# Small tiles for the scaled pairs, low parts by negated copies and accumulating loads, and folds of one block per step, in a decoder layer

## The chip, the cores and the metric

One core of one Trainium2 chip runs the whole layer in one launch. The metric is device time in microseconds (us). The kernel before has a median of 760.0 us over 3 runs (757.77 to 762.58).

## The reference

A decoder layer over 512 rows of 1024 columns, in fp32: an adaLN-modulated input, two causal attention branches (forgetting attention and stick-breaking attention), their gated merge and output projection, a norm, then a gated MLP (2816 wide) with a causal convolution of width 3, and a second norm. The change touches the part behind the first norm:

```python
u2 = x * (1.0 + sc2) + sh2
h = _causal_depthwise_conv(u2 @ w_up, conv_w, conv_b)
h_gate, h_val = jnp.split(h, 2, axis=-1)
ffn_out = (jax.nn.silu(h_gate) * h_val) @ w_down
x = _layer_norm(DEEPNORM_ALPHA * x + (1.0 + gt2) * ffn_out, ln2_g, ln2_b)
```

## The kernel before

**Split matmuls.** Each fp32 product is made of three matmuls on rounded parts: high by high, high by low, low by high. A weight tile arrives as fp32 (`raw`); ACT copies it rounded (the high part: `wh`, `wdh`), and DVE subtracts that from the original (the low part: `wl`, `wdl`, at L91).

**Items and the ring.** All weights of the layer's second half stand in one list of items (`add_item`), each with a source, a function that prepares it and its columns. `weights(i, ahead)` (L145 on) issues loads from SP in the list's order into a ring of 5 tiles `raw` (items of 512 columns, `rl`, go to a ring of 4 of their own in a late pool) and prepares `ahead` items beyond the one asked for. SP's order is the order of the code; the order of the other engines is made by a scheduler at build time. Each engine works through its own order strictly.

**Up projection.** A loop over 44 tiles n (L1097 on): 24 matmuls of 512 columns into one PSUM bank, which ACT (L1122) and DVE (L1123, L1124) evacuate together with the convolution. Six of the eight banks hold early products of the down projection, so two are left for this loop.

**Down projection.** It is a product of 2 x 2 blocks with seven multiplications (Strassen-like, in the Winograd form), over 11 pairs of 256 hidden channels. The rows of `wdp` hold the blocks of each pair as b11, b12, b22, b21 (512 columns each). Sums of weight blocks are formed by accumulating loads on POOL's queue (L160) and by `pair_proc`, and stored to DRAM as `t13`. B22 times the gate, the *scaled pairs*, is stored to DRAM as `wgt`: pairs 2 to 10 in `pair_proc` by an ACT DMA (L952), pairs 0 and 1 by two items of their own, listed at n = 17 and 21, that load 512 columns into a tile of the ring, multiply in place (L960, DVE) and store on POOL's queue (L961).

**The final stage** has four phases, each for both row blocks i = 0, 1 of the quadrant at hand: Z and then V (bank pairs `Z`, `W1`) over the two halves of `t13`; X over B21, whose six items are numbered 0 to 5 here (two pairs each, the last one pair); W over `wgt`: two streamed items for pairs 0 to 2, and eight *late items* (`rl`) for pairs 3 to 10, used by 24 matmuls of 512 columns for row block 2 and 48 of 256 columns for row block 3. Between them DVE *folds* the phases' banks into the residual `r` (tiles `xn`), times the gate halves `g0`, `g1`: `gated` (L1153 to L1155), called from `z_mark`, `v_mark`, `x_mark` and `w_mark` after each item. `first_rows` makes the second norm of row blocks 0 and 1 and stores them on POOL's queue (L1172); `tail` does so for blocks 2 and 3 at the end, with SP's stores.

Of the kernel before, what the change touches and what calls it, by code (L numbers as in the profile page):

```python
# [16 lines left out]
P = 128  # L17
# [6 lines left out]
FP = FT // 2  # L24
# [13 lines left out]
AHEAD = 2  # L38
NSPLIT = 3
LATE = 8  # L40
EARLY = 2
GS = 9
SS = 10
# [7 lines left out]
def layer_kernel(ctx: ExitStack, tc: tile.TileContext, out, xT, x, cT, crow, wa0, wa1, bcol, bgt, w1, wct, wv, bf,  # L51
# [18 lines left out]
    def nm(s):  # L70
        cnt[0] += 1
        return f"{s}_{cnt[0]}"
# [56 lines left out]
    def z(dt, s, shape=(P, 512)):  # L129
        return zp.tile(list(shape), dt, name=nm(s), tag="z", bufs=NZ)  # L130
# [8 lines left out]
    state = {"load": 0, "proc": 0}  # L139
    items, depth = [], [LOADS - 1]  # L140
    def add_item(src, proc, cols=1024):
        items.append([src, proc, cols, None, None])
        return len(items) - 1

    def weights(i, ahead=AHEAD):  # L145
        while state["load"] < min(len(items), i + depth[0]):
            it = items[state["load"]]
            if it[2] == 512:
                it[3] = state["late"].tile([P, 512], F32, name=nm("rl"), tag="rl", bufs=4)
            else:  # L150
                it[3] = stg.tile([P, 1024], F32, name=nm("raw"), tag="raw", bufs=LOADS)
            c = 0
            for src in it[0] if isinstance(it[0], list) else [it[0]]:
                w = src.shape[-1]
                d = nc.sync.dma_start(it[3][:, c : c + w], src)
# [210 lines left out]
    gated = []  # L366
# [202 lines left out]
    gt = [None, None]  # L569
# [81 lines left out]
    def split_cols(cols):  # L651
        def f(r):
            return split_proc(r, cols)
        return f
# [148 lines left out]
    last = hd[heads[1]]['last']  # L803
    for n, (b, h) in enumerate(heads):
        f1, f2, f3 = FILL[n // 8]
        if n + 2 < 16:
# [5 lines left out]
            last = hd[heads[n + 1]].get("last")  # L812
# [117 lines left out]
    def raw_proc(r):  # L930
        return r

    def halves_proc(r):
# [23 lines left out]

    def scale_proc(p):
        def f(r):
            V.tensor_tensor(r[:, 0:512], r[:, 0:512], gt[1][:, 512:1024], ALU.mult)  # L960
            G.dma_start(wgt[p], r[:, 0:512])  # L961
        return f

    wui, pi, wai = [], [], {}
# [22 lines left out]
    def add_late():  # L987
        if len(cli) < LATE:
            cli.append(add_item(wgt[FP - LATE + len(cli)], halves_proc, 512))

    def add_two(n, src, p, end):
        ws = [src(q) for q in range(p, min(p + 2, end))]
        n.append(add_item(ws, split_cols(512 * len(ws))))

    for p in range(0, FP - 1, 2):
        add_two(zi, lambda q: t13[q][:, 512:1024], p, FP - 1)
        if p == 0:
            add_pair_items(FP - 1)
            add_pair_sums(FP - 1)
    for p in range(0, FP - 1, 2):  # L1000
        add_two(vi, lambda q: t13[q][:, 0:512], p, FP - 1)
        if p > 2:
            add_late()
    for p in range(0, FP, 2):
        add_two(xi, lambda q: wdp[q][:, 1536:2048], p, FP)
        if p < 10:
            add_late()
# [27 lines left out]
    hs, ops, s4s = [], [], []  # L1035
# [61 lines left out]
    for n in range(2 * FT):  # L1097
        if n < NSPLIT:
            h, l = items[wui[n]][4]
# [41 lines left out]
    fin = ctx.enter_context(tc.tile_pool(name="fin", bufs=1, reuse_waits="tile"))  # L1141

    def fine(s):
        return fin.tile([P, 512], F32, name=nm(s), tag="fz", bufs=10)

    state["late"] = fin
    r = x1
    g0, g1 = gt[1][:, 0:512], gt[1][:, 512:1024]

    def half(w, e):  # L1150
        return [t[:, e * 512 : (e + 1) * 512] for t in w]

    def gated(i, e, t, src, op=ALU.add):  # L1153
        V.tensor_tensor(t, src, (g0, g1)[e], ALU.mult)
        V.tensor_tensor(r[i][e], r[i][e], t, op)  # L1155


    def stat_tile():
        return cons.tile([P, 3, 6], F32, name=nm("st"), tag="st3", bufs=2)
# [11 lines left out]
            V.scalar_tensor_tensor(v, v, rs, lnr[1][:, c], ALU.mult, ALU.add)  # L1171
            eng.dma_start(out[tb, c], v)  # L1172

    p1, u2, q1, u3, c22 = [[fine(n) for _ in range(2)] for n in ("p1", "u2", "q1", "u3", "c22")]

    def phase(ps, idx, end, take, mark, last=None):
        for n, k in enumerate(idx):
            w = weights(k)
            for a, p in enumerate(range(2 * n, min(end, 2 * n + 2))):
                t = take(p)  # L1180
                for i in range(2):
                    product(ps[i], t[:, top[i]], t[:, bot[i]], *half(w, a), p == 0, p == FP - 1)
            mark(n)
        if end < FP:
            t = take(end)
            for i in range(2):
                product(ps[i], t[:, top[i]], t[:, bot[i]], *[v[last] for v in state["t13"]], False, True)
            mark(len(idx))

    def g_part(c):  # L1190
        def f(p):
            t = ops[p][2][c]
            ops[p][2][c] = None
            return t
        return f

    def z_mark(n):
# [12 lines left out]
        if n < 5:  # L1210
            for p in range(max(GS, 2 * n + 2), min(FP, 2 * n + 4)):
                ready(p)

    def v_mark(n):
        for p in range(max(SS, 2 * n), min(FP, 2 * n + 2)):
            ops[p][3] = halves(ops[p][3])
        if n == 0:
            for i in range(2):
                V.tensor_tensor(q1[i], q1[i], Z[i], ALU.add)
                V.tensor_tensor(u3[i], u2[i], Z[i], ALU.add)  # L1220
        if n in (1, 2):
            gated(n - 1, 0, q1[n - 1], q1[n - 1])

    def first_rows(i):
        st = stat_tile()
# [16 lines left out]

    lnr = lnr2
    Z = [bank() for _ in range(2)]
    phase(Z, zi, FP - 1, g_part(0), z_mark, 1)
    W1 = [bank() for _ in range(2)]
    phase(W1, vi, FP - 1, g_part(1), v_mark, 0)
    X = [bank() for _ in range(2)]
    phase(X, xi, FP, lambda p: ops[p][1], x_mark)
# [101 lines left out]
```

## Time and profile before

| | |
|---|---|
| median of 3 runs | 760.0 us (757.77 to 762.58) |
| profiled execution | 760.22 us, its span 758.4 us, granted TensorE clock 0.996 |
| PE (matmuls) | 736.6 us busy, 97% of the span, 3478 matmuls |
| DVE | 608.5 us, 80% |
| ACT | 384.8 us, 51% |
| POOL | 108.5 us, 14% |
| DMA of the hardware queue for loads and stores | 37602 packets, 112.09 MB |
| DMA of POOL's queue | 2576 packets, 7.41 MB |

The span is what the profiler saw of the execution; 1.8 us lie around it. Rows of the profile name engine, line, operation and tiles as output<-inputs; a time in brackets at a row's end is the engine's idle time before it and what ended it. Rows of the waits give the waiting engine and line, what it waited for, us in total, the number of times, and the longest. Rows of stretches give, after the stretch, its length, the busy us of PE, its weight loads, DVE, ACT and POOL, then PE's granted clock, the share of time that DMA engines were busy, and GB/s.

### The profile page before, as it was taken

Reading aid. Unit: us, or ns where it says so; the run is one execution under the profiler, and the core shown is the slowest. Engines: PE = TensorE matmul, PEld = TensorE weight load, DVE = VectorE, ACT = ScalarE, POOL = GpSimd, SP = SyncE. Lnnn points to the kernel's source line nnn. Section 1 sums busy time; section 2 is a strip of 40 time slices with the busy share of each in tenths; the row PEclk is TensorE's granted clock in tenths of the full one; section 3 lists DMA queues with packets and bytes.
Section 4 is the critical chain, followed back from the end, with each engine's and each line's share of the span. In section 5 each row is a group of like instructions: output and inputs, shape, how many; then the busy total and the mean of one; then the engine's idle time right before and its main releaser. Section 6 shows DMA issues by size and latency. Waiting matters only on the chain.

```text
span 758.4 us, 9876 instructions
## 1 busy us (share of the span) xinstructions
PE 736.6 (97%) x3478; PEld 607.2 (80%) x3478; DVE 608.5 (80%) x1017; ACT 384.8 (51%) x678; POOL 108.5 (14%) x138
## 2 busy tenths in 40 slices
PE   8999999999999999999999999999899999999993
PEld 4878888878888888788889888877688888887883
DVE  6869799887888895864687889876886687669997
ACT  4566566685866654432055563443454355446530
POOL 1026223452010011462000000000000000000010
PEclk9999999999999999999999999999999999999998
DMA  9943446313432232542074777667774674567711
GB/s 323 406 174 116 162 168 219 114 58 119 161 112 82 86 128 78 183 144 83 1 250 111 259 227 233 198 193 208 246 234 159 193 223 144 167 189 249 225 68 56
DMA packets 43252, 128.01 MB, mean 169 GB/s; under 512 B 5665, under 2 KB 6177, under 8 KB 43202
## 3 DMA queue, kind: packets, MB, share of 16 engines
q1 hardware_dynamic: 37602, 112.09, 42.4%
q0 software_dynamic: 2576, 7.41, 5.0%
q10 hardware_dynamic: 3024, 7.88, 3.0%
q8 instruction: 27, 0.44, 0.2%
q14 instruction: 23, 0.19, 0.1%
HBM read 117.07 MB, written 10.22 MB: 168 GB/s over the span
## 4 chain that ended last, share of the span: by engine, by line
PE 66%; DVE 13%; DMA 12%; issue 6%; ACT 2%; SPq 0%; ACTq 0%; POOL 0%; DVEq 0%; POOLq 0%
PE ps L135 14%; PE ps L133 14%; PE ps L134 14%; PE ps L300 5%; DVE wl L91 3%; DMA raw<-in_wdp 3%; PE ps L551 2%; PE ps L533 2%; PE ps L892 2%; PE ps L891 2%; PE ps L893 2%; DMA raw<-in_wup 2%; DMA raw<-in_wa 1%; PE ps L1075 1%; PE ps L1076 1%
## 5 line engine op out<-in xcount | busy, mean ns | idle before, releaser
L91 DVE TENSOR_TENSOR wl<-raw,wh 128x1024 fp32r<-128x1024 f32 (+2 forms) x112 | 139.9, 1249 | 57.7 <-ACT wh L181 57.3
L181 ACT ACTIVATE wh<-raw 128x1024 fp32r<-128x1024 f32 (+1 forms) x103 | 108.4, 1053 | 138.0 <-PE ps L134 63.9
L133 PE MATMUL ps<-u2h,wh 128*128 128x512 f32 (+1 forms) x376 | 141.9, 377 | 2.6 <-DVE cv L1124 2.5
L135 PE MATMUL ps<-u2h,wl 128*128 128x512 f32 (+1 forms) x376 | 141.3, 376 | 0.0
L134 PE MATMUL ps<-u2l,wh 128*128 128x512 f32 (+1 forms) x376 | 141.2, 376 | 0.0
L133 PEld LDWEIGHTS ps<-u2h,wh 128*128 128x128 f32 x376 | 70.8, 188 | 17.5 <-issue 4.8
L135 PEld LDWEIGHTS ps<-u2h,wl 128*128 128x128 f32 x376 | 70.8, 188 | 12.9
L134 PEld LDWEIGHTS ps<-u2l,wh 128*128 128x128 f32 x376 | 70.8, 188 | 12.6
L133 PE MATMUL ps<-uh,wh 128*128 128x512 f32 x200 | 79.4, 397 | 0.0
L135 PE MATMUL ps<-uh,wl 128*128 128x512 f32 x200 | 78.3, 391 | 0.9 <-DVE wl L91 0.9
L134 PE MATMUL ps<-ul,wh 128*128 128x512 f32 x200 | 78.2, 391 | 0.0
L160 POOL DMA_DIRECT2D raw<-in_wdp x11 | 9.5, 865 | 271.8 <-DVE raw L946 96.1
L135 PEld LDWEIGHTS ps<-uh,wl 128*128 128x128 f32 x200 | 37.6, 188 | 9.5 <-DVE wl L91 1.4
L513 POOL TENSOR_TENSOR pt<-pt,om 128x127 f32<-128x127 f32 (+3 forms) x32 | 43.2, 1361 | 8.0 <-DVE om L512 8.0
L133 PEld LDWEIGHTS ps<-uh,wh 128*128 128x128 f32 x200 | 37.6, 188 | 7.3
L134 PEld LDWEIGHTS ps<-ul,wh 128*128 128x128 f32 x200 | 37.7, 188 | 7.2
L1122 ACT ACTIVATE cv<-ps,cw 128x512 f32<-128x512 f32 x44 | 33.5, 766 | 16.5 <-PE ps L135 10.4
L1123 DVE SCALAR_TENSOR_TENSOR cv<-ps,cw,cv 128x511 f32<-128x511 f32 x44 | 32.6, 744 | 5.4 <-ACT cv L1122 5.4
L1130 ACT ACTIVATE cv<-cv 128x512 f32<-128x512 f32 x22 | 13.9, 630 | 39.2 <-DVE cv L1124 39.2
L1124 DVE SCALAR_TENSOR_TENSOR cv<-ps,cw,cv 128x510 f32<-128x510 f32 x44 | 32.5, 742 | 0.2
L632 POOL TENSOR_TENSOR raw<-raw,gt 128x1024 f32<-128x1024 f32 x8 | 21.3, 2669 | 67.6 <-DMA raw<-in_wo 54.5
L512 DVE TENSOR_TENSOR_SCAN om<-om,dg 128x127 f32<-128x127 f32 (+3 forms) x32 | 29.6, 981 | 0.5 <-ACT om L507 0.4
(226 smaller groups left out, 1606.7 us busy)
## 6 DMA issues: line engine op xcount, KB each, us to landing
raw<-in_wup SPq DMA_DIRECT2D x44, 512.0 KB, 4.5
raw<-in_wa SPq DMA_DIRECT2D x32, 512.0 KB, 4.2
raw<-in_wct SPq DMA_DIRECT2D x25, 512.0 KB, 3.8
raw<-in_wdp SPq DMA_DIRECT2D x22, 512.0 KB, 5.5
wa<-in_wa SPq DMA_DIRECT2D x14, 512.0 KB, 7.9
raw<-in_wdp SPq DMA_DIRECT2D x24, 256.0 KB, 5.2
raw<-in_wdp POOLq DMA_DIRECT2D x11, 512.0 KB, 7.8
t<-raw ACTq DMA_DIRECT2D x10, 512.0 KB, 4.1
```

Of the source, the lines that this page charges most:

```text
L91: state["read"] = V.tensor_tensor(o, i, fl(hi), ALU.subtract)
L133: PE.matmul(ps, wh, ah, start=first, stop=False)
L134: PE.matmul(ps, wh, al, start=False, stop=False)
L135: return PE.matmul(ps, wl, ah, start=False, stop=last)
L181: state["hi"] = S.activation(h[:, 0:cols], r[:, 0:cols], AF.Copy)
L300: PE.matmul(grp[g], w, u, start=j == 0 and n == 0, stop=j == KT - 1 and n == (1 if g == 7 else 2))
L512: V.tensor_tensor_scan(d0, d0, dg[:, 513 - (e - s) : 512][:, ::-1], 0.0, ALU.mult, ALU.max)
L513: G.tensor_tensor(pt[b][:, s : e - 1], pt[b][:, s : e - 1], om[:, s + 1 : e], ALU.mult)
L632: G.tensor_tensor(r, r, gt[0], ALU.mult)
L1122: S.activation(t, ps, AF.Identity, bias=cw[:, n, 3:4], scale=cw[:, n, 2:3])
L1123: V.scalar_tensor_tensor(t[:, 1:], ps[:, 0:511], cw[:, n, 1:2], t[:, 1:], ALU.mult, ALU.add)
L1124: V.scalar_tensor_tensor(t[:, 2:], ps[:, 0:510], cw[:, n, 0:1], t[:, 2:], ALU.mult, ALU.add)
```

## The change

1. The two items of scaled pairs 0 and 1 are listed at n = 15 and 19, and load into tiles of 512 columns from the general pool (`z`), as all `rl` tiles now do. The late pool keeps 8 work tiles where it had 10.
2. For items 1, 3 and 5 of X and both streamed items of W, the low part is made in another way: ACT copies the rounded high part once more with the sign turned, and a DMA on POOL's queue loads the source again, adding to it. High and low parts get tiles of their own, `xh` and `xl`, two of each.
3. Folds go one block per step, each directly from its bank, and spread over more steps; they take 34 operations of 512 columns where there were 30.

The tuples SENT_V, SENT_W and HELD_Z are empty, and HELD_V and HELD_X place the late items where they were.

```diff
@@ weights
             if it[2] == 512:
-                it[3] = state["late"].tile([P, 512], F32, name=nm("rl"), tag="rl", bufs=4)
+                it[3] = z(F32, "rl")
@@ preparing an item
+    def sent_split(srcs):
+        def f(r):
+            cols = 512 * len(srcs)
+            h = state["fin"].tile([P, 1024], F32R, name=nm("xh"), tag="xh", bufs=2)
+            l = state["fin"].tile([P, 1024], F32R, name=nm("xl"), tag="xl", bufs=2)
+            hi_of(h[:, 0:cols], r[:, 0:cols])
+            S.activation(l[:, 0:cols], fl(h[:, 0:cols]), AF.Copy, scale=-1.0)
+            for a, src in enumerate(srcs):
+                G.dma_start(l[:, a * 512 : a * 512 + 512], src, accum_op=ALU.add)
+            return h, l
+        return f
...
     def scale_proc(p):
         def f(r):
-            V.tensor_tensor(r[:, 0:512], r[:, 0:512], gt[1][:, 512:1024], ALU.mult)
-            G.dma_start(wgt[p], r[:, 0:512])
+            V.tensor_tensor(r, r, gt[1][:, 512:1024], ALU.mult)
+            G.dma_start(wgt[p], r)
         return f
@@ the list of items
-        if n in (17, 21):
-            add_item(wdp[n // 4 - 4][:, 1024:1536], scale_proc(n // 4 - 4))
+        if n in (15, 19):
+            p = (15, 19).index(n)
+            add_item(wdp[p][:, 1024:1536], scale_proc(p), 512)
...
     for p in range(0, FP, 2):
-        add_two(xi, lambda q: wdp[q][:, 1536:2048], p, FP)
-        if p < 10:
-            add_late()
+        add_two(xi, lambda q: wdp[q][:, 1536:2048], p, FP, p // 2 in SENT)
+        add_late(p // 2 in HELD_X)
     for p in range(0, FP - LATE, 2):
-        add_two(wi, lambda q: wgt[q], p, FP - LATE)
+        add_two(wi, lambda q: wgt[q], p, FP - LATE, p // 2 in SENT_I)
@@ folds
-    def gated(i, e, t, src, op=ALU.add):
+    def fold(i, e, t, src, op=ALU.add):
         V.tensor_tensor(t, src, (g0, g1)[e], ALU.mult)
         V.tensor_tensor(r[i][e], r[i][e], t, op)
@@ z_mark
+        if n in (4, 5):
+            fold(n - 2, 0, p1[n - 4], p1[n - 4])
@@ v_mark
-        if n == 0:
-            for i in range(2):
-                V.tensor_tensor(q1[i], q1[i], Z[i], ALU.add)
-                V.tensor_tensor(u3[i], u2[i], Z[i], ALU.add)
-        if n in (1, 2):
-            gated(n - 1, 0, q1[n - 1], q1[n - 1])
+        if n in (0, 1):
+            fold(2 + n, 1, v2[n], u2[n], ALU.subtract)
+        if n in (2, 3):
+            for t, ps in zip((q1, u2)[n - 2], Z):
+                V.tensor_tensor(t, t, ps, ALU.add)
+        if n in (4, 5):
+            fold(n - 4, 0, q1[n - 4], q1[n - 4])
@@ x_mark
         if n == 0:
             for i in range(2):
-                V.tensor_tensor(c22[i], u3[i], W1[i], ALU.add)
-                V.tensor_tensor(u2[i], u2[i], W1[i], ALU.add)
+                fold(i, 1, u2[i], u2[i], ALU.subtract)
         if n in (1, 2):
-            gated(n - 1, 1, c22[n - 1], c22[n - 1], ALU.subtract)
+            fold(n - 1, 1, v2[n - 1], W1[n - 1], ALU.subtract)
+            V.tensor_tensor(r[n + 1][1], r[n + 1][1], v2[n - 1], ALU.subtract)
...
-        if n == 4:
-            for i in range(2):
-                gated(2 + i, 1, u2[i], u2[i], ALU.subtract)
@@ w_mark
-                V.tensor_tensor(p1[i], p1[i], X[i], ALU.add)
-                gated(2 + i, 0, p1[i], p1[i])
+                fold(2 + i, 0, p1[i], X[i])
```

Three places of the engines' orders show what moves. The first is SP's queue around the load of scaled pair 1. Before (`raw_4955` is the scaled pair, in the ring; the number behind a tile's name tells tiles apart):

```order
L155 DMA raw_4896<-in_wup 128x1024
L155 DMA raw_4898<-in_wa 128x1024
L155 DMA raw_4953<-in_wup 128x1024
L155 DMA raw_4955<-in_wdp 128x512
L155 DMA raw_5018<-in_wdp 128x1024
L155 DMA raw_5060<-in_wdp 128x512
L155 DMA raw_5062<-in_wup 128x1024
L155 DMA raw_5118<-in_wdp 128x1024
```

With the change:

```order
L162 DMA raw_4908<-in_wup 128x1024
L162 DMA rl_4910<-in_wdp 128x512
L162 DMA raw_4912<-in_wup 128x1024
L162 DMA raw_4955<-in_wa 128x1024
L162 DMA raw_4957<-in_wup 128x1024
L162 DMA raw_5020<-in_wdp 128x1024
L162 DMA raw_5023<-in_wdp 128x512
L162 DMA raw_5066<-in_wup 128x1024
```

The scaled pair (`rl_4910`) moved ahead by an up weight and an adaLN weight, and no tile of the ring is given to it.

The second place is the end of POOL's queue, which before held only the four stores `out` behind the last accumulating load of a pair sum. With the change:

```order
L167 DMA raw_6217<-in_wdp 128x1024
L957 DMA xl_6660<-in_wdp 128x512 x2
L957 DMA xl_6719<-in_wdp 128x512 x2
L957 DMA xl_6789<-in_wdp 128x512
L957 DMA xl_6822<-wgt_72 128x512
L957 DMA xl_6822<-wgt_73 128x512
L957 DMA xl_6828<-wgt_74 128x512
L1196 DMA out<-xn_3489 128x512
```

Eight accumulating DMAs came in, for items 1, 3 and 5 of X and for W's two items.

The third place is PE at the change from X to W. Before (`wdh`, `wdl` are a late item's parts, 256 columns of row block 3; after these two rows 46 more such matmuls follow before the first with `wl_6813`):

```order
L1074 MATMUL ps_6826<-wh_6812,hv_4191 128x512
L1074 MATMUL ps_6827<-wh_6812,hv_4191 128x512
L1074 MATMUL ps_6896<-wdh_6544,hv_4886 128x256
L1075 MATMUL ps_6896<-wdl_6545,hv_4886 128x256
...
L1075 MATMUL ps_6826<-wl_6813,hv_4191 128x512
L1076 MATMUL ps_6826<-wh_6812,hv_4191 128x512
```

With the change:

```order
L1103 MATMUL ps_6838<-xh_6821,hv_4191 128x512
L1103 MATMUL ps_6839<-xh_6821,hv_4191 128x512
L1103 MATMUL ps_6906<-wdh_6544,hv_4902 128x256
L1104 MATMUL ps_6906<-wdl_6545,hv_4902 128x256
L1105 MATMUL ps_6906<-wdh_6544,hv_4902 128x256
L1103 MATMUL ps_6906<-wdh_6588,hv_5128 128x256
L1104 MATMUL ps_6838<-xl_6822,hv_4191 128x512
L1105 MATMUL ps_6838<-xh_6821,hv_4191 128x512
```

Only 4 matmuls of row block 3 now stand ahead of W's first low part, and 4 more ahead of its second item's. Block 2's 24 matmuls (into `ps_6838`) follow W directly, and the remaining 40 matmuls of 256 columns come last; before, block 2's 24 were the last.

More of the change, by code (lines that the diff above doesn't have):

```diff
@@ L40 @@
 LATE = 8
+SENT_V = ()
+SENT = (1,3,5)
+SENT_W = ()
+SENT_I = (0,1)
+HELD_Z = ()
+HELD_V = (2,3,4)
+HELD_X = (0,1,2,3,4)
 EARLY = 2
@@ L931, in raw_proc, with sent_proc, f @@
         return r
+    def sent_proc(src):
+        def f(r):
+            h, l = z(F32R, "wdh"), z(F32R, "wdl")
+            hi_of(h, r)
+            S.activation(l, fl(h), AF.Copy, scale=-1.0)
+            G.dma_start(l, src, accum_op=ALU.add)
+            return h, l
+        return f
+    def sent_split(srcs):
+        def f(r):
+            cols = 512 * len(srcs)
[5 more added lines that the diff above has]
+                G.dma_start(l[:, a * 512 : a * 512 + 512], src, accum_op=ALU.add)
+            return h, l
+        return f
     def halves_proc(r):
@@ L985, in layer_kernel, with add_late, add_two @@
     zi, vi, xi, cli, wi = [], [], [], [], []
[L987 to L991, printed above, removed]
+    def add_late(yes):
+        if yes:
+            src = wgt[FP - LATE + len(cli)]
+            cli.append(add_item(src, sent_proc(src) if len(cli) in SENT_W else halves_proc, 512))
+    def add_two(n, src, p, end, sent=False):
         ws = [src(q) for q in range(p, min(p + 2, end))]
-        n.append(add_item(ws, split_cols(512 * len(ws))))
+        n.append(add_item(ws, sent_split(ws) if sent else split_cols(512 * len(ws))))
     for p in range(0, FP - 1, 2):
@@ L999, in layer_kernel @@
             add_pair_sums(FP - 1)
+        add_late(p // 2 in HELD_Z)
     for p in range(0, FP - 1, 2):
-        add_two(vi, lambda q: t13[q][:, 0:512], p, FP - 1)
-        if p > 2:
-            add_late()
+        add_two(vi, lambda q: t13[q][:, 0:512], p, FP - 1, p // 2 in SENT_V)
+        add_late(p // 2 in HELD_V)
     for p in range(0, FP, 2):
-        add_two(xi, lambda q: wdp[q][:, 1536:2048], p, FP)
-        if p < 10:
-            add_late()
+        add_two(xi, lambda q: wdp[q][:, 1536:2048], p, FP, p // 2 in SENT)
+        add_late(p // 2 in HELD_X)
     for p in range(0, FP - LATE, 2):
-        add_two(wi, lambda q: wgt[q], p, FP - LATE)
+        add_two(wi, lambda q: wgt[q], p, FP - LATE, p // 2 in SENT_I)
     def up_mm(ps, h, l, ts):
@@ L1143, in fine @@
     def fine(s):
-        return fin.tile([P, 512], F32, name=nm(s), tag="fz", bufs=10)
-    state["late"] = fin
+        return fin.tile([P, 512], F32, name=nm(s), tag="fz", bufs=8)
+    state["fin"] = fin
     r = x1
@@ L1151, in half @@
         return [t[:, e * 512 : (e + 1) * 512] for t in w]
-    def gated(i, e, t, src, op=ALU.add):
-        V.tensor_tensor(t, src, (g0, g1)[e], ALU.mult)
-        V.tensor_tensor(r[i][e], r[i][e], t, op)
     def stat_tile():
@@ L1172, in tail, with phase @@
             eng.dma_start(out[tb, c], v)
-    p1, u2, q1, u3, c22 = [[fine(n) for _ in range(2)] for n in ("p1", "u2", "q1", "u3", "c22")]
-    def phase(ps, idx, end, take, mark, last=None):
+    p1, u2, q1, v2 = [[fine(n) for _ in range(2)] for n in ("p1", "u2", "q1", "v2")]
+    def phase(ps, idx, end, take, mark, ahead, last=None):
         for n, k in enumerate(idx):
-            w = weights(k)
+            w = weights(k, ahead)
             for a, p in enumerate(range(2 * n, min(end, 2 * n + 2))):
@@ L1195, in g_part @@
         return f
+    def fold(i, e, t, src, op=ALU.add):
+        V.tensor_tensor(t, src, (g0, g1)[e], ALU.mult)
+        V.tensor_tensor(r[i][e], r[i][e], t, op)
     def z_mark(n):
```

6 lines of the change are left out of this document (3 added, 3 removed).

## The prediction

> **What bounds the kernel now.** I read the page's head first, then busy time by stretches of 20 us, the waits of the stretches in which PE loses time, and the rows in order of time there.
>
> ```profile
> span 758.4 us, 9876 instructions
> PE 736.6 (97%) x3478; PEld 607.2 (80%) x3478; DVE 608.5 (80%) x1017; ACT 384.8 (51%) x678; POOL 108.5 (14%) x138
> ...
> 500.00:520.00 20.00, 19.38 (x84) 15.24 (x83) 17.41 (x29) 10.17 (x18) 1.43 (x2) 1.00 0.54 137
> 520.00:540.00 20.00, 18.19 (x78) 14.48 (x79) 13.20 (x23) 9.28 (x16) 0.00 (x0) 1.00 0.69 237
> 540.00:560.00 20.00, 19.48 (x84) 15.24 (x83) 15.17 (x24) 8.51 (x13) 0.85 (x1) 1.00 0.83 278
> 560.00:580.00 20.00, 20.00 (x90) 16.57 (x89) 15.24 (x26) 9.43 (x16) 0.86 (x1) 1.00 0.61 191
> ...
> 700.00:720.00 20.00, 20.00 (x90) 16.57 (x89) 20.00 (x29) 10.76 (x15) 0.00 (x0) 1.00 0.74 240
> 720.00:740.00 20.00, 18.98 (x106) 16.52 (x106) 20.00 (x40) 5.79 (x8) 2.22 (x4) 1.00 0.19 66
> 740.00:760.00 20.00, 7.00 (x31) 5.45 (x30) 13.49 (x33) 0.48 (x2) 0.00 (x0) 0.80 0.15 53
> ```
>
> PE bounds: 97% of the span, and the change issues the same 3478 matmuls. What a change of this kind can win are PE's few holes (500 to 560, and one at 737) and what follows PE's last matmul. From 700 to 740 DVE is full too (20.00 of 20); it sets the hole at 737 and the end.
>
> First the holes of the up projection (waits of 480 to 560, then rows of it; the last number in a wait's row is the longest):
>
> ```profile
> ACT wh L181 <- DMA raw<-in_wup: 16.8, 4, 6.0
> ACT ln L1119 <- DMA ln<-in_lnrow: 4.8, 1, 4.8
> PE ps L133 <- DVE cv L1124: 2.5, 4, 1.6
> ...
> SPq L155 <- DMA wgt<-raw: 11.4, 2, 5.9
> ...
> 515.02 0.58 POOL L961 DMA_DIRECT2D wgt<-raw  x1 [1.05 <-DVE raw L960]
> 522.97 0.33 SPq L155 DMA_DIRECT2D raw<-in_wdp  x1
> 523.74 2.98 SPq L155 DMA_DIRECT2D raw<-in_wup  x2
> 528.71 1.06 ACT L181 ACTIVATE wh<-raw 128x1024 fp32r<-128x1024 f32 x1 [3.09 <-DMA raw<-in_wup]
> 531.94 0.74 DVE L1124 SCALAR_TENSOR_TENSOR cv<-ps,cw,cv 128x510 f32<-128x510 f32 x1
> 532.83 0.47 PE L133 MATMUL ps<-u2h,wh 128*128 128x512 f32 x1 [1.64 <-DVE cv L1124]
> ```
>
> A chain: the scaled pair's store is issued at 515.02 from a slot of the ring; SP stands until it has landed (one of two such waits, 11.4 us together), issues its load at 522.97 and the next up weights behind it at 523.74; ACT, in order, waits for them until 528.71, so the evacuation behind it ends late on DVE and PE lacks a bank until 532.83.
>
> A stall costs more than the idle time of its row, because a matmul's row (0.39) is longer than its step (0.227):
>
> ```profile
> 509.19 0.39 PE L135 MATMUL ps<-u2h,wl 128*128 128x512 f32 x1
> 509.98 0.47 PE L133 MATMUL ps<-u2h,wh 128*128 128x512 f32 x1 [0.41 <-DVE cv L1124]
> 510.29 0.39 PE L134 MATMUL ps<-u2l,wh 128*128 128x512 f32 x1
> ...
> 520.03 0.47 PE L133 MATMUL ps<-u2h,wh 128*128 128x512 f32 x1 [0.25 <-DVE cv L1124]
> ...
> 549.59 0.47 PE L133 MATMUL ps<-u2h,wh 128*128 128x512 f32 x1 [0.19 <-DVE cv L1124]
> ```
>
> From 509.19 to 510.29 there are 1.10 us instead of 0.45: 0.64 lost. By starts, the same working gives 0.48 at 520.03, 1.88 at 532.83, 0.38 at 538.69 and 1.3 from 545.9 to 549.9: 4.7 in all, of which 3.4 lie in the first four.
>
> **Part 1, the scaled pairs in small tiles.** The two loads get tiles of 512 columns outside the ring, so no later weight load waits for a store's landing: the two SP waits go. The first four stalls (3.4 us) stand in the 50 us behind these waits, and I give them to the waits whole. The fifth stall stands behind ACT's wait of 4.8 us for the second norm's row; in the new order that ACT operation comes after the evacuation that it now holds up. I count 0.8 of the 1.3. Sum: -4.2. Bounds: -1.5 (other reasons for late up weights remain: DMA engines are 0.54 to 0.83 busy here) and -4.7 (all).
>
> **Part 2, low parts by accumulation.** Five items (three of B21, two of W) lose their low-part subtraction on DVE and get a second ACT operation and eight DMAs of 256 KB on POOL's queue.
>
> ```profile
> L91 DVE TENSOR_TENSOR wl<-raw,wh 128x1024 fp32r<-128x1024 f32 x12 | 14.6, 1215 | 0.0
> L91 DVE TENSOR_TENSOR wl<-raw,wh 128x512 fp32r<-128x512 f32 x2 | 1.3, 654 | 0.0
> L181 ACT ACTIVATE wh<-raw 128x1024 fp32r<-128x1024 f32 x10 | 10.6, 1060 | 12.3 <-PE ps L1076 11.1 <-issue 1.2
> L181 ACT ACTIVATE wh<-raw 128x512 fp32r<-128x512 f32 x2 | 1.3, 634 | 1.2 <-PE ps L1076 1.1
> L1155 DVE TENSOR_TENSOR xn<-xn,c 128x512 f32<-128x512 f32 x2 | 1.4, 678 | 0.0
> ```
>
> Records of DVE overlap by some 0.08, so steps are 1.13 (1024 columns) and 0.60 (512). DVE loses 3 x 1.13 + 2 x 0.60 = 4.6; ACT gains 3 x 1.06 + 2 x 0.63 = 4.5, which its idle time covers (16.6 busy of the 40 us from 700). POOL's queue holds nothing else there except, behind the eight, the four stores of finished rows, which nobody waits for.
>
> The unknown is L, the time from the issue of an item's first accumulating DMA until the pair has landed. Rows to bound it (names as listed: issues, KB each, median us to landing; then the spread of the 512 KB accumulating loads, and of the stores of rows by SP and POOL):
>
> ```profile
> raw<-in_wdp POOLq DMA_DIRECT2D x11, 512.0 KB, 7.8
> out<-xn POOLq DMA_DIRECT2D x4, 256.0 KB, 2.4
> ...
> DMA to landing us min/median/max: 6.3/7.8/8.9
> ...
> DMA to landing us min/median/max: 2.0/2.3/2.5
> ```
>
> Above: 8.9, the longest of POOL's accumulating loads, which move as many bytes as a pair. Below: 3.1, two quiet stores issued 0.6 apart. The operation is that of the first row, the empty DMA engines (share 0.19 after 720) are those of the second: I take 6.0 for W and, with share 0.74 before 720, 6.9 for B21.
>
> PE's needs, in the time of the old trace:
>
> ```profile
> 711.40 1.06 ACT L181 ACTIVATE wh<-raw 128x1024 fp32r<-128x1024 f32 x1 [0.83 <-PE ps L1076]
> ...
> 730.24 0.62 PE L1074 MATMUL ps<-wh,hv 128*128 128x512 f32 x2
> 730.69 0.28 PE L1074 MATMUL ps<-wdh,hv 128*128 128x256 f32 x1
> 730.81 0.28 PE L1075 MATMUL ps<-wdl,hv 128*128 128x256 f32 x1
> ...
> 737.62 0.50 PE L1075 MATMUL ps<-wl,hv 128*128 128x512 f32 x1 [1.02 <-DVE wl L91]
> ```
>
> X has 66 matmuls of 0.227 and ends at 730.24, so it starts at 715.28, its item 1 at 718.00.
> - Item 1 (first use of the new tiles): ACT can copy at about 711.1, POOL issues at 713.2; PE wants the pair's second half at 719.6. Stall L - 6.4 = 0.5.
> - W's first item must wait until X's item 3 has left one of two tiles; then two copies of 1.06 and the semaphores, 2.25 to the DMA. Until PE wants the second half there are 18 steps of X, 2 of W, 4 half-width ones (0.12) and 5 steps: 6.16. Stall 2.25 + L - 6.16 = 2.1. W's second item (two copies of 0.63, one DMA) starts at the end of X and is wanted 4.1 plus this stall later: hidden.
> - X's items 2 and 4 keep their subtraction, but folds now stand ahead of it on the full DVE: adding steps up I get 722.0 against PE's need at 721.6, and 727.9 against 727.5. Taken 0.9, bounds 0 and 2.
>
> Sum 3.5, against the hole at 737 that goes (1.02 idle, 1.2 by starts): PE's end moves from 747.0 to 749.3, +2.3. If ACT's copies lost their cover, up to 4.5 would come on top.
>
> **Part 3, folds and the end.** One block per step makes 34 operations of 30: +4 x 0.60, so DVE is 2.2 lighter in all and by adding up steps it has caught up by 742. What counts is the order: the whole-width matmuls of block 2 now come ahead of block 3's last 40 half-width ones.
>
> ```profile
> 747.04 0.69 DVE L1277 TENSOR_TENSOR xn<-xn,ps 128x512 f32<-128x512 f32 x1 [1.43 <-PE ps L1076]
> ...
> 753.49 1.54 DVE L1171 SCALAR_TENSOR_TENSOR xn<-xn,mv,ln 128x512 f32<-128x512 f32 x3
> ```
>
> Now both blocks' norms follow PE's end: 8.0 us of DVE, then 3.4 of SP's stores. Then block 2's part runs under those 40 matmuls (4.8 us): its operations come to some 5.2 by the steps of the old tail (0.60 to 0.73 for 512 columns, 0.07 to 0.24 for the small ones), so 0.4 stays, and block 3's own add, statistics and scaling come to 4.1: 4.5. Gain -3.5; bounds -2.5 (block 2 late by another microsecond) and -4.
>
> **Sum.** -4.2 + 2.3 - 3.5 = -5.4 on the profiled execution (760.2; span 758.4, 1.8 around it): 754.8. The median is 0.2 under that execution: 754.6.
>
> **Rivals.**
> - Quick accumulation. If a pair lands in 3.1 like the stores of rows, both L stalls are gone: +2.3 becomes 0.9 - 1.2 = -0.3, and the median 752.0; with the whole 4.7 of part 1 and no late folds 750.6. For it: empty DMA engines after 720. Against: none of the 11 accumulating loads was under 6.3. [...]
> - Other waits hold the up weights. Part 1 gives 1.5 alone: 757.3. For it: ACT waited for up weights four times, SP for stores twice.
> - Starved accumulation, the slower side. From 700 to 740 DVE has no gap; if POOL gets its descriptors out only between DVE's operations, each of a pair's two issues is late by up to 1.2 (the subtraction's row), L is 8.9 + 2.4 = 11.3, and the stalls at X's item 1 and W's first item are 4.9 and 7.4. With 0.9 they make 13.2 - 1.2 = +12.0, less 7.7: 764.3. It decides from L = 9.2 on, where 2L - 10.3 + 0.9 - 1.2 uses up 7.7. Against: the stores of rows issued from 732.0 to 735.5, under the same full DVE, landed in 2.0 to 2.5. [...]
>
> **How the numbers follow.** Forecast, L from 5 to 7.5: 0.52. Quick: 0.25. Other waits: 0.13. Starved: 0.10. Within the forecast L = 8.9 would give 759.6, L = 5 about 753. About 1% (7.6 us) is what a measurement of this kernel can tell from no change: below 752.4 lies most of the quick case and the forecast's edge, 0.28; above 767.6 only the worst of the last, 0.07; 0.65 between. The range, 751.0 to 760.5, leaves out the lower edge of the quick case and most of the starved one.
>
> **What would show it.** Right: SP no longer waits for the scaled pairs' store; PE's busy time from 500 to 540 is within 0.5 of 40; the accumulating DMAs land 4.5 to 7 after issue; PE waits about 2 us for the low part of W's first item; 4.5 us from PE's last matmul to DVE's last operation. Wrong: accumulations of over 9 us, ACT still idle for up weights by 3 us and more, or both norms still behind PE's end.

## The result, and the profile after

The changed kernel takes as long as the one before: 759.87 us (757.35 to 761.67) against 758.38 us (756.5 to 762.58), medians of 22 runs each, ratio 1.0011 with a 95% interval of 0.9998 to 1.0023. Measured again beside the experiments it was 1.0013 (1.0001 to 1.0024). Forecast was 754.6.

The two profiled executions say otherwise: 757.37 us (span 755.6) against 760.22 (758.4). The one of before lies 1.8 above its kernel's median, the one of after 2.5 below. For both offsets the runs below offer a cause. First the profile after: its head, and busy time by stretches, to set beside the rows of before.

```profile
span 755.6 us, 9896 instructions
...
500.00:520.00 20.00, 20.00 (x90) 16.57 (x89) 17.46 (x29) 9.52 (x16) 1.43 (x2) 1.00 0.77 221
520.00:540.00 20.00, 20.00 (x90) 16.58 (x89) 17.94 (x30) 10.28 (x18) 0.86 (x1) 1.00 0.68 222
540.00:560.00 20.00, 19.96 (x89) 16.24 (x88) 13.17 (x21) 10.94 (x18) 0.85 (x1) 1.00 0.72 231
...
700.00:720.00 20.00, 17.72 (x77) 14.05 (x77) 20.00 (x32) 12.59 (x18) 3.51 (x4) 1.00 0.94 262
720.00:740.00 20.00, 17.74 (x82) 14.36 (x81) 17.05 (x36) 5.83 (x9) 5.70 (x8) 1.00 0.49 112
740.00:760.00 20.00, 6.99 (x50) 6.43 (x48) 9.76 (x26) 0.59 (x2) 0.00 (x0) 0.80 0.15 53
```

PE's holes between 500 and 560 are gone: 59.96 of 60 us where 57.05 were. In their place PE now stands 4.5 us between 700 and 740, where it had stood 1.0. The share of busy DMA engines from 700 to 720 rose from 0.74 to 0.94. Who makes PE wait, in the waits from 655 on and in rows of POOL and PE in order of time:

```profile
PE ps L1104 <- DMA xl<-in_wdp: 2.3, 2, 1.5
PE ps L1104 <- DMA xl<-wgt: 2.3, 2, 1.8
...
709.09 1.75 POOL L957 DMA_DIRECT2D xl<-in_wdp  x2 [51.26 <-ACT xl L955]
715.76 0.47 PE L1104 MATMUL ps<-xl,hv 128*128 128x512 f32 x1 [1.49 <-DMA xl<-in_wdp]
717.96 0.50 PE L1104 MATMUL ps<-xl,hv 128*128 128x512 f32 x1 [0.80 <-DMA xl<-in_wdp]
...
727.31 1.75 POOL L957 DMA_DIRECT2D xl<-wgt  x2 [5.43 <-ACT xl L955]
731.61 0.47 PE L1104 MATMUL ps<-xl,hv 128*128 128x512 f32 x1 [1.79 <-DMA xl<-wgt]
733.47 0.50 PE L1104 MATMUL ps<-xl,hv 128*128 128x512 f32 x1 [0.47 <-DMA xl<-wgt]
```

All four waits are for accumulating loads, for the two halves of X's item 1 and for those of W's first item. Item 1's pair is issued at 709.09 and PE goes on with its second half at 717.96, almost 9 us later. By starts (gap less the step of 0.227 or 0.12) these waits cost 2.8 in X and 2.8 in W. The end, in rows of PE and DVE:

```profile
746.71 0.28 PE L1105 MATMUL ps<-wdh,hv 128*128 128x256 f32 x1
...
742.24 0.69 DVE L1304 TENSOR_TENSOR xn<-xn,ps 128x512 f32<-128x512 f32 x1 [3.86 <-PE ps L1105]
747.62 0.41 DVE L1304 TENSOR_TENSOR xn<-xn,ps 128x256 f32<-128x256 f32 x1
750.70 1.54 DVE L1195 SCALAR_TENSOR_TENSOR xn<-xn,mv,ln 128x512 f32<-128x512 f32 x3
```

Block 2's norm starts at 742.24, under the half-width matmuls; block 3's takes from 747.62 to 752.24, 4.6 us. It has to wait for the rest of block 2's, so DVE's last operation ends 5.25 us behind PE's last matmul (746.99), where it ended 8.0 behind it: 2.8 shorter. PE itself ends where it did (746.99 against 747.00). In these two profiles the new waits have used up what the holes gave, and the difference of the spans, 2.8 us, is the end.

### The profile page after: what moved, and what is told of

The parts are those of the page before. It is cut to its first block, busy times and chain, and to the rows that moved or that the text cites. A ratio compares the mean times of both kernels' runs of the same rounds, so it can differ in the third digit from the quotient of the medians.

```text
span 755.6 us, 9896 instructions
## 1 busy us (share of the span) xinstructions
PE 735.8 (97%) x3478; PEld 607.9 (80%) x3478; DVE 604.9 (80%) x1016; ACT 389.9 (52%) x683; POOL 115.7 (15%) x146
## 4 chain that ended last, share of the span: by engine, by line
PE 84%; DVE 7%; DMA 5%; ACT 2%; issue 2%; POOL 0%; DVEq 0%; SPq 0%; ACTq 0%
PE ps L142 18%; PE ps L140 18%; PE ps L141 18%; PE ps L307 5%; PE ps L1104 3%; PE ps L1105 3%; PE ps L1103 3%; PE ps L558 2%; PE ps L540 2%; PE ps L900 2%; PE ps L898 2%; PE ps L899 2%; DVE wl L98 1%; PE ps L481 1%; PE ps L482 1%
## 5 line engine op out<-in xcount | busy, mean ns | idle before, releaser
L98 DVE TENSOR_TENSOR wl<-raw,wh 128x1024 fp32r<-128x1024 f32 (+2 forms) x107 | 134.0, 1254 | 50.9 <-ACT wh L188 50.7
L188 ACT ACTIVATE wh<-raw 128x1024 fp32r<-128x1024 f32 x98 | 104.0, 1061 | 112.3 <-PE ps L141 58.3
```

The source lines that it names most:

```text
L98: state["read"] = V.tensor_tensor(o, i, fl(hi), ALU.subtract)
L188: state["hi"] = S.activation(h[:, 0:cols], r[:, 0:cols], AF.Copy)
```

## The experiments

Each was timed beside the kernel before, in 5 to 12 runs; ratios are to that kernel on the same chip, and need not agree with the quotient of the medians to the last digit.

**Are the two profiles typical?** The first two runs repeat the kernels unchanged. Before, again:

> The kernel before, unchanged, for the granted clock and span of its runs and a second profile. Three theories of why 4.7 us won in the up projection do not show in the medians. Clock: a fuller PE is granted less clock; then this kernel's runs show a higher mean clock (0.995 and more) than the changed kernel's (0.991 to 0.996, by 0.003 or some 2 us in the mean), and at equal clock it is about 2.8 us slower. Untypical profile: the holes between 500 and 560 us of the profiled execution (4.7 us) are not in most runs; then a second profile shows under 2 us of them and a span of 755 to 756.5 at clock 0.996. Stalls: the accumulating loads alone ate the gain; then clock and holes are as before, and the runs lie around 760 at the clock of 0.996.

758.16 us (755.25 to 761.17). Its second profile has a span of 755.6 us, and smaller holes:

```profile
500.00:520.00 20.00, 20.00 (x90) 16.57 (x89) 17.11 (x29) 8.60 (x16) 1.43 (x2) 1.00 0.65 200
520.00:540.00 20.00, 19.72 (x87) 15.68 (x86) 15.77 (x26) 9.28 (x16) 0.85 (x1) 1.00 0.72 231
540.00:560.00 20.00, 19.55 (x84) 15.26 (x83) 13.97 (x23) 10.56 (x16) 0.02 (x1) 1.00 0.70 227
```

By starts they cost 2.0 us, where the first profile had 4.7. So the holes differ from run to run, and the profile on which the forecast stood had them larger. The mean clock of this kernel's runs is 0.995. The changed kernel, again:

> The changed kernel, unchanged, beside the others on one chip. All theories: within 1 us of the first measurement relative to before (ratio 1.000 to 1.002). A second profile shows whether its four waits for xl (1.5, 0.8, 1.8, 0.5 us idle) and its 4.5 us tail return: all theories say within 0.5 us each. Clock theory: its mean clock is below that of the kernel before by 0.002 or more.

759.16 us, and a mean clock of 0.993. Its profile caught an execution at 0.991. Rows of PE there, then stretches of 3.41 us (PE's granted clock is the third number from the end) of this execution, and last such stretches of the first profile after:

```profile
714.72 0.47 PE L1104 MATMUL ps<-xl,hv 128*128 128x512 f32 x1 [1.75 <-DMA xl<-in_wdp]
...
716.72 0.63 PE L1104 MATMUL ps<-xl,hv 128*128 128x512 f32 x1 [0.60 <-DMA xl<-in_wdp]
717.15 0.63 PE L1105 MATMUL ps<-xh,hv 128*128 128x512 f32 x1
717.58 0.63 PE L1103 MATMUL ps<-xh,hv 128*128 128x512 f32 x1
...
720.70 0.40 PE L1105 MATMUL ps<-wh,hv 128*128 128x512 f32 x1
720.93 0.39 PE L1103 MATMUL ps<-wh,hv 128*128 128x512 f32 x1
```

```profile
713.52:716.93 3.41, 1.60 (x6) 1.07 (x7) 3.41 (x6) 0.00 (x0) 0.05 (x1) 1.00 1.08 276
716.93:720.35 3.42, 3.42 (x9) 2.65 (x9) 3.42 (x7) 1.23 (x2) 0.00 (x0) 0.50 0.92 198
720.35:723.76 3.41, 3.41 (x16) 2.80 (x16) 3.41 (x6) 0.04 (x1) 0.86 (x1) 1.00 0.41 66
730.59:734.00 3.41, 1.66 (x6) 1.13 (x7) 3.30 (x10) 0.19 (x2) 2.00 (x3) 1.00 0.92 135
734.00:737.41 3.41, 3.41 (x11) 2.74 (x11) 3.41 (x6) 0.00 (x0) 1.08 (x2) 0.50 0.98 334
```

```profile
712.06:715.48 3.42, 2.22 (x10) 1.50 (x8) 3.42 (x7) 2.76 (x4) 1.75 (x2) 1.00 0.94 175
715.48:718.89 3.41, 2.33 (x9) 1.66 (x10) 3.41 (x6) 0.00 (x0) 0.00 (x0) 1.00 1.09 294
729.13:732.54 3.41, 1.62 (x10) 1.29 (x9) 3.29 (x11) 1.26 (x3) 1.75 (x3) 1.00 0.82 144
```

Behind the waits of item 1 the granted clock is half from 716.93 to 720.35, behind those of W from 734.00 to 737.41, and matmuls start every 0.43 us instead of every 0.227. The waits of item 1 are about the same size in both executions (1.75 and 0.60 against 1.49 and 0.80); only here did the clock fall.

The traces show what differs. Here the granted clock changes at 716.93, 720.35, 734.00 and 737.41, that is 3.42, 13.65 (four times 3.41) and 3.41 us apart. The stretches of the first profile after are of that length too, counted back from the fall of its clock at 749.61, behind PE's end. In the 3.41 us ahead of the two falls here PE was busy, by its rows, for 1.60 and 1.66 us; ahead of two falls in runs below for 1.65 (idle work in front of W) and 1.02 (item 1 alone). The clock held behind 1.62 in the first profile after (the last row above) and behind 1.78 in the first profile before (530.06 to 533.48), so the busy time of a stretch does not part the two cases sharply. Item 1's two waits lie in one stretch here; in the first profile after they lie in two, in which PE was busy for 2.22 and 2.33.

Each of the two falls here lasts 3.4 us and, with matmuls every 0.43 us instead of every 0.227, can cost about half of that, an estimate of 1.7. The mean clock of a run allows a rough count: of the changed kernel's 34 runs, 14 stand at 0.991 (taken as two falls; mean 760.2), 15 at 0.993 or 0.994 (one; 759.2) and 5 at 0.995 or 0.996 (none; 758.1). That is 1.3 falls, an estimate of 2.2 us, in the mean; by the groups' means a fall costs rather 1.1. The sorting is not sharp: the half clock behind PE's end set in 2.9 us after the start of the last matmul in the first profile after (746.71 to 749.61) and 5.3 in the first profile before (746.61 to 751.93), and by an estimate these 2.4 us at half clock alone move the mean of a run of 757 us by 0.0016, where a fall of 3.41 moves it by 0.0023. The first profile was one of the five.

**The change in pieces.** Small tiles and their new places alone, everything else as before:

```diff
-                it[3] = state["late"].tile([P, 512], F32, name=nm("rl"), tag="rl", bufs=4)
+                it[3] = z(F32, "rl")
...
-        if n in (17, 21):
-            add_item(wdp[n // 4 - 4][:, 1024:1536], scale_proc(n // 4 - 4))
+        if n in (15, 19):
+            p = (15, 19).index(n)
+            add_item(wdp[p][:, 1024:1536], scale_proc(p), 512)
```

> Part 1 alone: the two scaled pairs in tiles of 512 columns at n = 15 and 19, everything else as before. All theories: PE's holes between 500 and 560 go from 4.7 to under 1 in the profile. Stalls theory: 3.5 to 4.5 us faster than before in the medians. Clock theory: the mean granted clock falls by 0.002 to 0.004 and the median gains 1 to 2 only. Untypical profile: the median gains 0 to 2 at an unchanged clock.

755.07 us (754.17 to 756.14), ratio 0.9960 (0.9945 to 0.9975): 3.1 us faster, between what the theories of stalls (3.5 to 4.5) and of an untypical profile (0 to 2) had expected, with a spread of 2 us instead of 6, at a mean clock of 0.995. Here the fuller PE was not granted less clock: the kernel before also has 0.995. The change without accumulation:

```diff
-SENT = (1,3,5)
+SENT = ()
-SENT_I = (0,1)
+SENT_I = ()
```

> The changed kernel with no accumulated low parts (both tuples empty): small tiles and the folds remain. PE's waits for xl (5.5 us by starts in the changed kernel's profile) go; DVE has 4.6 us more to do. Stalls theory: 2 to 4 us faster than the changed kernel. Rival, DVE: without the relief the full DVE makes PE wait for the low parts in X and W by as much, and it is within 1 us of the changed kernel. Clock theory: whatever PE wins here is given back at about half.

755.78 us, ratio 0.9963 (0.9950 to 0.9977). Accumulation therefore costs 3.4 us (759.16 less 755.78), and the folds, 755.78 less 755.07, have brought nothing clear of noise. The waits of PE from 700 on and rows of PE and DVE show why:

```profile
PE ps L1104 <- DVE wl L98: 2.1, 3, 1.1
...
717.28 0.50 PE L1104 MATMUL ps<-wl,hv 128*128 128x512 f32 x1 [1.13 <-DVE wl L98]
...
740.76 1.02 DVE L1304 TENSOR_TENSOR xn<-xn,ps 128x512 f32<-128x512 f32 x2 [0.86 <-PE ps L1105]
748.71 1.54 DVE L1195 SCALAR_TENSOR_TENSOR xn<-xn,mv,ln 128x512 f32<-128x512 f32 x3
```

The end is shorter here too, by less (DVE's last operation ends 6.4 us behind PE's last matmul, against 8.0 in the kernel with small tiles and places alone and 5.25 in the changed kernel). But the folds now stand ahead of low parts on a full DVE, and PE loses 3.9 us by starts at X's items.

Accumulation in X only, then in W only (the other tuple emptied):

> The changed kernel with accumulated low parts for X's items 1, 3 and 5 only; W's two items go by DVE's subtraction. Waits-and-clock theory: a wait of 2 us of PE for an accumulating load costs its idle time and, in most runs, some 3.4 us at half clock behind it. Here the waits at X's item 1 (2.8 us by starts) and the half clock behind them remain, those in W go: 755.5 to 757, mean clock 0.994 to 0.995. Rival, traffic alone: POOL's loads slow everything in X, then it stays at 758 and above.

> The changed kernel with accumulated low parts for W's two items only. With no X item in the two tiles, W's copies need not wait for item 3 of X, so the loads are issued early. Waits-and-clock theory: no wait for xl in W, clock 0.996 and above, DVE's waits of 3.9 us in X as in the kernel without any accumulation: 754 to 756. Rival, the accumulating load itself is too slow: W's wait of about 2 us stays and with it 757 to 759.

X only: 757.52 us, ratio 0.9984 (0.9971 to 0.9998), just above its expectation, mean clock 0.993, just below it; item 1 waits 2.91 and 0.59 idle, and the half clock follows (mean clock of this profile 0.993). W only: 755.20 us, ratio 0.9955 (0.9943 to 0.9967), clock 0.997: with no X item in the two tiles the loads start earlier, and one wait of 0.92 is left, where none was expected. Against no accumulation, by the ratios, X alone costs 1.6, W alone gains 0.6 and both together cost 3.8, each to within about 1.5 by the intervals. Some 2.8 of it appear only with both; that they arise where W's copies wait for tiles that X still holds (ACT's copies into `xh` waited 9.1 us for PE in the first profile) is argued, not tested by itself.

**Why item 1's pair is late.** Accumulation for that item alone, and for items 3 and 5 alone, each with `SENT_I = ()`:

```diff
-SENT = (1,3,5)
+SENT = (1,)
```

> The changed kernel with an accumulated low part for X's item 1 alone: no second pair follows on POOL's queue some 4 us later. Theory, POOL's pairs slow each other: the pair lands in 6 to 7 us and PE waits under 1 us at item 1, clock 0.996, 754.5 to 756. Rival, the DMA engines are full there (share 0.94 from 700 to 720, with the ring's own loads): it lands in 8 us and more, the wait of 2 to 3 us and the half clock behind it stay, 756.5 to 758.

```diff
-SENT = (1,3,5)
+SENT = (3,5)
```

> The changed kernel with accumulated low parts for X's items 3 and 5 alone, which are wanted 5 and 11 us later than item 1. Theory, an accumulating load costs nothing where it has 9 us and more: no wait for xl, no half clock (0.996 and above), and the relief of DVE shortens its waits late in X: 754 to 755.7. Rival: the loads of POOL hold up other loads, 756 and above.

Item 1 alone: 757.31 us, ratio 0.9991 (0.9979 to 1.0002), a wait of 2.39 idle and half clock from 715.5. Items 3 and 5: 755.59 us, ratio 0.9968 (0.9957 to 0.9979), no wait for `xl` at all. The landing times of the accumulating loads, in the changed kernel, with item 1 alone, and with items 3 and 5:

```profile
DMA to landing us min/median/max: 4.2/6.1/8.4
```

```profile
DMA to landing us min/median/max: 7.4/8.2/9.0
```

```profile
DMA to landing us min/median/max: 5.5/6.5/7.7
```

One pair with no other behind it on POOL's queue still takes 7.4 and 9.0, so the second pair is not what slows it. What is left, not tested, is the time in which it runs, when SP's loads share the DMA engines (POOL's queue alone took 0.41 of them from 709 to 718 in the first profile, SP's 0.57). Items 3 and 5 are not much quicker, but are wanted later.

**Does the wait bring the half clock?** The changed kernel with idle work in front of W (each repetition starts anew, so it changes no result):

```diff
+            if p == 0:
+                for i in range(2):
+                    for _ in range(5):
+                        PE.matmul(W[i], t[:, top[i]], half(w, a)[0], start=True, stop=True)
```

> The changed kernel with ten idle repetitions of W's first two matmuls ahead of them (each is started anew, so the result is the same): 2.3 us of PE work where PE waited 2 us for the accumulating load. Clock theory: the half clock behind this wait goes, since PE is busy; the runs show 0.993 to 0.996 (none at 0.991) and the median is 0.8 to 1.7 us below the changed kernel's. Rival, the half clock has nothing to do with the wait: clocks as in the changed kernel (0.991 to 0.996) and the same time or up to 0.5 us more.

758.27 us; ratio 1.0003 (0.9989 to 1.0016), against 1.0013 and 1.0011 for the changed kernel. Mean clock 0.995 instead of 0.993, and none of its 12 runs below 0.992, where 14 of 34 stood at 0.991. In its profile:

```profile
730.00 2.43 PE L1294 MATMUL ps<-xh,hv 128*128 128x512 f32 x10
...
732.88 0.47 PE L1104 MATMUL ps<-xl,hv 128*128 128x512 f32 x1 [0.23 <-DMA xl<-wgt]
...
733.00:735.00 2.00, 1.53 (x7) 0.92 (x7) 2.00 (x6) 0.00 (x0) 0.96 (x2) 1.00 1.03 163
735.00:737.00 2.00, 1.91 (x7) 1.31 (x8) 2.00 (x4) 0.00 (x0) 1.08 (x2) 1.00 0.94 320
```

PE goes on at the same point, 2.88 us after X, but works for most of that time, and the fall in W does not come; the one behind item 1 does, from 717.86. The clocks speak for the wait as the cause; the time alone (0.6 to 0.8 less by the ratios, with overlapping intervals) would not.

**What emptied the holes of the up projection.** The new tiles at the old places, and the new places with the old tiles:

```diff
-                it[3] = state["late"].tile([P, 512], F32, name=nm("rl"), tag="rl", bufs=4)
+                it[3] = z(F32, "rl")
...
-            add_item(wdp[n // 4 - 4][:, 1024:1536], scale_proc(n // 4 - 4))
+            p = (17, 21).index(n)
+            add_item(wdp[p][:, 1024:1536], scale_proc(p), 512)
```

> Part 1 without the move: the two scaled pairs in tiles of their own, but listed at n = 17 and 21 as before. Theory, the ring slot held by the store: the holes between 500 and 560 go as with both (part 1 alone: 755.1), 754.5 to 756. Rival, the place in the list: SP and ACT meet the scaled pair's load at a bad moment; then the holes stay, 757 to 759, and the spread of the runs stays at 5 us and more.

```diff
-        if n in (17, 21):
-            add_item(wdp[n // 4 - 4][:, 1024:1536], scale_proc(n // 4 - 4))
+        if n in (15, 19):
+            p = (15, 19).index(n)
+            add_item(wdp[p][:, 1024:1536], scale_proc(p))
```

> The move without the tiles: the two scaled pairs listed at n = 15 and 19, still in the ring of 5. Theory, the ring slot: SP still waits for the stores' landing, holes of 2 to 5 us, 757 to 759. Rival, the place: the holes go, 754.5 to 756.

Tiles alone: 757.51 us, ratio 0.9999 (0.9987 to 1.0011). Places alone: 755.00 us, ratio 0.9961 (0.9949 to 0.9974). The theory of the ring slot falls. With the tiles alone SP does not wait for a scaled pair's store any more, and yet ACT and PE stand (rows of ACT, then PE):

```profile
544.62 0.63 ACT L88 ACTIVATE wdh<-raw 128x512 fp32r<-128x512 f32 x1 [3.20 <-DMA raw<-in_wdp]
...
550.62 1.06 ACT L181 ACTIVATE wh<-raw 128x1024 fp32r<-128x1024 f32 x1 [2.13 <-DMA raw<-in_wup]
553.24 1.06 ACT L181 ACTIVATE wh<-raw 128x1024 fp32r<-128x1024 f32 x1 [1.56 <-DMA raw<-in_wup]
...
557.35 0.47 PE L133 MATMUL ps<-u2h,wh 128*128 128x512 f32 x1 [1.78 <-DVE cv L1125]
```

At n = 17 and 21 the list also has the two items of the next pair's sums, so the scaled pair makes it three loads between two up weights; at 15 and 19 nothing else is loaded. Two more runs, both in the old ring, tell "earlier" from "not in the crowd": n = 19 and 23 (free, later) and n = 16 and 20 (earlier by one, with one adaLN weight there).

> As the move alone, still in the ring of 5, but later instead of earlier: listed at n = 19 and 23, where no other item stands between two up weights. Theory, the crowded place: at n = 17 and 21 the scaled pair makes three loads in a row between two up weights, so the second up weight lands late; in any free place the holes go: 754.5 to 756. Rival, earlier is what helps: then here they stay, 757 to 759.

> Earlier by one tile only: listed at n = 16 and 20, behind the adaLN weight that stands there, so two loads in a row between up weights before two more. Crowded-place theory: between the free place and the old one, 755.5 to 757.5. Rival, earlier is what helps: 754.5 to 755.5.

754.97 us, ratio 0.9956 (0.9942 to 0.9971), and 754.57 us, ratio 0.9954 (0.9937 to 0.9971). Later does as well as earlier, and so does a place with one neighbour. There the crowded-place theory had expected 755.5 to 757.5 and was too high: of the places tried only the one with three in a row costs. In the second, waits of SP and stretches:

```profile
SPq L155 <- DMA wgt<-raw: 10.1, 2, 6.6
...
500.00:520.00 20.00, 20.00 (x90) 16.58 (x89) 17.73 (x29) 9.90 (x17) 1.43 (x2) 1.00 0.78 232
520.00:540.00 20.00, 20.00 (x90) 16.57 (x89) 17.36 (x31) 9.75 (x17) 0.86 (x1) 1.00 0.68 221
540.00:560.00 20.00, 20.00 (x90) 16.57 (x89) 14.81 (x25) 11.10 (x19) 0.85 (x1) 1.00 0.80 253
```

SP waits for the stores for 10.1 us, nearly as long as before (11.4), and PE has no hole.

**A faster version.** Small tiles in the new places, the old folds, and accumulation for W's items only, in tiles that X never holds:

```diff
...
+            h = state["fin"].tile([P, cols], F32R, name=nm("xh"), tag=f"xh{cols}", bufs=1)
+            l = state["fin"].tile([P, cols], F32R, name=nm("xl"), tag=f"xl{cols}", bufs=1)
...
-        add_two(wi, lambda q: wgt[q], p, FP - LATE)
+        add_two(wi, lambda q: wgt[q], p, FP - LATE, True)
```

> Small tiles (part 1), the old folds, and accumulated low parts for W's two items in tiles of their own; block 2's matmuls follow W and the 48 half-width ones come last, by the scheduler. Against part 1 alone (755.1): PE's hole of 1.2 us before W's low part goes and the tail of 8 us of DVE becomes about 4.5 to 5. Waits-and-clock theory: 750.5 to 753, the fastest so far. Rival, DVE is the bound at the end: the folds of the old order come due only after X, block 2's norm slips behind them, and it stays at 754 to 755.

752.95 us (752.52 to 753.55), ratio 0.9929 (0.9917 to 0.9941), faster than both. In rows of POOL, PE and DVE:

```profile
720.79 1.75 POOL L941 DMA_DIRECT2D xl<-wgt  x2 [65.77 <-ACT xl L939]
724.97 0.47 PE L1088 MATMUL ps<-xl,hv 128*128 128x512 f32 x1 [0.54 <-DMA xl<-wgt]
727.38 0.50 PE L1088 MATMUL ps<-xl,hv 128*128 128x512 f32 x1 [0.80 <-DMA xl<-wgt]
...
741.10 0.28 PE L1089 MATMUL ps<-wdh,hv 128*128 128x256 f32 x1
...
745.89 1.54 DVE L1184 SCALAR_TENSOR_TENSOR xn<-xn,mv,ln 128x512 f32<-128x512 f32 x3
```

The scheduler, with W's low parts off DVE, puts block 3's half-width matmuls last by itself; DVE's last operation ends 6.05 us behind PE's last matmul, nearer to the changed kernel's 5.25 than to the 8.0 before, without its folds; X has no wait, and in this profile the clock does not fall before PE's end.

## Why the prediction failed

In medians the change goes: small tiles and places -3.1, folds and order +0.7, accumulation +3.4, together +1.0. The forecast's sum was -5.4. Part 1 makes 1.1 of the difference of 6.4. Parts 2 and 3 make the other 5.3: forecast at -1.2 together, measured at +4.1. The steps that failed there are the time of X's accumulating loads, taken too short, and the price of a wait, taken as its idle time with nothing for the clock behind it.

- **Part 1** (-4.2): the size was near (-3.1, by the ratio's interval -1.9 to -4.2), the cause was not. "I give them to the waits whole" is the step of this part that failed: SP's two waits stood ahead of the holes in time, and were taken for their cause, but they come back (10.1 us) without a hole. What brings the holes is the place with three loads in a row between two up weights. And 4.7 us was a large draw: the second profile had 2.0.
- **Part 2, L in W**: taken 6.0, PE went on with the second half 6.2 after the issue; stall forecast 2.1, idle 1.79 and 0.47, by starts 2.8. Near.
- **Part 2, L in X**: taken 6.9, PE went on with the first half 6.7 after the issue, with the second 8.9; stall forecast 0.5, cost 2.8. The choice of 6.9 failed, and the bound of 8.9 held only just here: it was 9.5 with the idle work and 9.6 with item 1 alone. The share of busy DMA engines rose from 0.74 to 0.94 with the accumulating loads, and I weighed L by the old share.
- **Part 2, low parts late by 0.9**: did not come.
- **What no term held**: the half clock, by the rough count 2.2 us in the mean. In neither profile of the kernel before was a wait of PE followed by it; I priced a wait at its idle time. In the repeated run of the changed kernel 1.75 and 0.60 us idle were followed by 3.4 us at half clock where most of both lay in one stretch of 3.41 us; 1.49 and 0.80 in two stretches were not.
- **Part 3** (-3.5): the end became 2.8 shorter, inside the bounds; block 2 kept 0.6 of DVE behind PE's end, not 0.4, and block 3 took 4.6, not 4.1. But without the relief the new folds cost PE 3.9 in X, so folds and order alone bring nothing. The forecast counted DVE's lighter load and did not price the order in which the folds stand ahead of low parts.
- **The rivals**: quick accumulation did not come; the shortest accumulating load in the changed kernel took 4.2. Starvation by DVE did not come either: in the faster version DVE had no gap from 718 to 728, and the loads issued there landed in 4.1 to 6.0. "Other waits hold the up weights" was right as to the cause, wrong as to what remains.
- **The median**: I took the median 0.2 under the profiled execution, from three runs. Over 22 runs it was 1.8 under.

Open: why the clock fell behind a stretch with 1.66 us of busy PE and held behind one with 1.62. Between three loads in a row and the holes the chain was read in profiles, not taken apart further. That X's pair is slowed by SP's loads is what is left after the second pair was excluded; SP's loads were not taken away. The nearest to it are W's loads: in the first profile after no other queue moved a packet from 727 to 734, and they landed in 4.2 to 5.6 us; in the faster version they landed in 4.1 to 6.0.

## What to carry to other kernels

Waits of PE cost more here than their idle time: behind 1.75 and 0.60 us idle at X's item 1 the granted clock was half for 3.4 us, and again behind the wait in W. So look at the granted clock behind each wait, in more than one execution, and keep PE busy with other matmuls until the late operand is there; with the idle work the fall in W did not come. The accumulating loads moved work off a full engine without a long wait only where they were issued far enough ahead: PE went on 8.9 to 9.6 us after the issue of X's first pair, beside SP's loads, and 6.2 to 6.6 after that of W's, without them; put such a load where the tiles are free early, not where the engine is fullest. And a wait that stands ahead of a hole is not yet its cause: move the item and keep the wait, or take the wait and leave the item, before the hole is priced.

## What the runs showed of the hardware

In the repeated run of the changed kernel the granted clock of TensorE fell to 0.50 at 716.93 and at 734.00, for 3.42 and 3.41 us, behind 3.41 us in which PE was busy for 1.60 and 1.66. It fell at 717.86 with the idle work, behind 1.65 of busy PE, and at 715.5 with item 1 alone, behind 1.02. It held behind 1.62 in the first profile after and behind 1.78 in the first profile before. The accumulating loads of X's item 1 (256 KB each, POOL's queue) landed 6.5 and 8.3 us after their issue in the first profile after, and 7.4 and 9.0 with item 1 alone, beside SP's loads; those of W landed in 4.2 to 5.6 in the first profile after, where no other queue moved a packet (727 to 734) and POOL's queue kept the DMA engines busy for 0.62 of the time. Stores of the same size on the same queue took 2.3 to 2.5 us in the kernel before when no other queue moved data (730 to 740), and 6.2 and 7.9 in the up projection.
